# A pool of their own for the convolved rows, merge adds on VectorE, most weight roundings on ScalarE

## Chip, cores and metric

The kernel runs on one core of one Trainium2 chip. The metric is the device time of one execution in microseconds. The words used below: TensorE (PE in the rows, PEld its weight loads), VectorE (DVE), ScalarE (ACT), GpSimd (POOL) and SyncE's queue of transfers (SP).

## What is computed

One step of a trunk layer on 1088 frames (1024 of a prompt, 64 of a sample) of width 1024, in fp32. Four token mixers work side by side, their outputs are gated and added, and a gated feed-forward part with a causal convolution follows. The part that matters here:

```
p = x @ w_in + b_in                       # columns for the mixers A, B, C, D
mix = sum over m of sigmoid(x @ w_mg[m] + b_mg[m]) * (y_m @ w_br[m])
x1 = layer_norm(ALPHA * x + mix @ w_out)
gate = x1 @ w_ff_gate ; up = x1 @ w_ff_up          # 1024 -> 2048
ffn = (gelu(causal_dwconv3(gate)) * up) @ w_ff_down
x2 = layer_norm(ALPHA * x1 + ffn)
```

## The kernel before

**Weights.** Each fp32 product is made of three products of rounded parts: high by high, high by low, low by high (`mm3`, L293). The 184 weight tiles of 512 KB are listed in `plan` in the order of use, with a key each: `in` (48, the projection), `mg` (32, the gates of the merge), `br` (16, the branches), `out` (8), `fg` and `fu` (32, feed-forward gate and up) and `fd` (48, down). `wissue` (L246) loads a tile into `wr` (two buffers) on SyncE's queue, rounds it to `wh` (three buffers), and VectorE forms the remainder `wl` (L262). The rounding is on ScalarE for `fg` and `fu` (L259), on GpSimd for all others (L261).

**Merges.** The mixers run in the order D, C, B, A, each followed by its merge (`merge`, L672). Gates come out of TensorE as `psd` and ScalarE takes their tanh into `th` (L668). Then a tile `br` gives `psm` (two banks), and VectorE forms `(th + 1) * psm` in three pieces (L703). From the second merge on, the sum of the earlier mixers is loaded into `prev` and GpSimd adds it (L705), 24 times in all. After the last merge the sum is turned into the rounded parts `mixh` and `mixl` for the output projection (L1457, L1458).

**Feed-forward.** The columns are taken as 16 tiles `f` of 128. Tiles 0 and 1 are made plainly: gates (`ff_gate`), the convolution (`conv`, L1559 to L1567, into a tile `cv`), then the up products, which `put_up` multiplies into `cv` straight from the banks (L1547) and stores to `h_d`. For tiles 2 to 15, two at a time, `pair` (L341) replaces eight products of half matrices by seven. It needs sums of blocks of `x1` (`xsums`, L322: four sums `xs`, each as a rounded part on ScalarE at L338 and a remainder on VectorE at L339, per slice `k` of four) and sums of the weights (`wsums`, L269: `st`, `sh`, `sl`). The last 320 columns of each tile, `rest` (L357), and the first two products need no sums. All of it is on line L354 in the rows.

**What sets the order.** The program is written as generators that a tile scheduler orders; each engine then works through its list in order. Tiles come from pools; a tile waits until what used its memory before is done. `slot_pool` closes the pool of the slots and opens a new one in the same memory; here it opens the pools of the sums (`x`, `w`, `p`) beside seven slots, after the up tiles of `f` = 0 and 1.

Of the kernel before, what the change touches and what calls it, by code (L numbers as in the profile page):

```python
# [19 lines left out]
P = 128  # L20
# [48 lines left out]
def trunk_kernel(ctx: ExitStack, tc: tile.TileContext, I, O, dbg=None):  # L69
# [39 lines left out]
    def nm(s):  # L109
        uid[0] += 1  # L110
        return f"{s}_{uid[0]}"

    def slot(shape=(P, T), dt=F32, s="t"):
        return slots[1].tile(list(shape), dt, tag="T", name=nm(s))
# [4 lines left out]
    def bank(tag, n=512):  # L119
        return ps1.tile([P, n], F32, tag=tag, name=nm("ps" + tag))  # L120
# [125 lines left out]
    def wissue(upto, pin=False):  # L246
        while wptr[0] <= min(upto, len(plan) - 1):
            key, ap, a = plan[wptr[0]]
            pool = wide["f"] if key[0] == "fd" and key[1] > 2 and key[1] % 2 == 0 else wp
            raw = pool.tile([P, a, 1024 // a], F32, tag="wr", name=nm("wr"), bufs=2)  # L250
            pinned(SP.dma_start(raw, ap), pin)
            if key[0] == "out" and (key[1] == 1 or key[2] == 3):
                h = slot([P, a, 1024 // a], F32R, "woh")
                l = slot([P, a, 1024 // a], F32R, "wol")
            else:
                h = pool.tile([P, a, 1024 // a], F32R, tag="wh", name=nm("wh"), bufs=3)
                l = pool.tile([P, a, 1024 // a], F32R, tag="wl", name=nm("wl"), bufs=3)
            if key[0] in ("fg", "fu"):
                S.activation(h, raw, AF.Copy)  # L259
            else:  # L260
                G.tensor_scalar(h, raw, 1.0, 1.0, OP.mult, OP.mult)  # L261
            V.tensor_sub(l, raw, h.bitcast(F32))  # L262
            wtiles[key] = (h, l)
            wraw[key] = raw
            wptr[0] += 1
            if key in pairs:
                wsums(wraw.pop(pairs[key]), wraw.pop(key), key)
# [54 lines left out]
    def xsums():  # L322


        for j in (0, 1, 3):
            xs[j] = tuple(wide["x"].tile([P, 4, 384], F32R, tag=f"x{j}{i}", name=nm("xs"), bufs=1) for i in range(2))
        xs[2] = tuple(t[1][:, 0:4, :] for t in (xh, xl))

        for k in range(4):
            t, b12, b22, b21 = [wide["p"].tile([P, 384], F32, tag="xf", name=nm("xf"), bufs=5) for _ in range(4)]  # L330
            for v, c, kk in ((t, 0, k), (b12, 1, k), (b22, 1, k + 4), (b21, 0, k + 4)):
                V.tensor_tensor(v, xh[c][:, kk, :].bitcast(F32), xl[c][:, kk, :].bitcast(F32), OP.add)
            V.tensor_tensor(t, b12, t, OP.subtract)
            V.tensor_tensor(b12, b22, b12, OP.subtract)
            V.tensor_tensor(b22, b22, t, OP.subtract)
            V.tensor_tensor(b21, b21, b22, OP.subtract)
            for j, v in ((0, t), (1, b22), (3, b21), (2, b12)):
                S.activation(xs[j][0][:, k, :], v, AF.Copy)  # L338
                V.tensor_sub(xs[j][1][:, k, :], v, xs[j][0][:, k, :].bitcast(F32))  # L339

    def pair(ka, kb, add, put):  # L341

# [51 lines left out]
    def run(*gens):  # L394
        for g in gens:
            for _ in g:
                pass
# [274 lines left out]
    def merge(m, it):  # L672
# [19 lines left out]
        def br(e):  # L692
            wh, wl = wget(("br", m, e))
            for g in range(2):
                th = ths.pop((m, e + g))
                if it > 0:
                    prev = slot([P, T], F32, "prev")
                    SP.dma_start(prev, mx_d[it - 1][e + g])
                for c, (n0, n) in enumerate(CH):
                    ps = bank("m")  # L700
                    mm3(ps[:, :n], [(wh[:, k, g * P:(g + 1) * P], wl[:, k, g * P:(g + 1) * P],
                                     yh[k][:, n0:n0 + n], yl[k][:, n0:n0 + n]) for k in range(4)])
                    V.scalar_tensor_tensor(th[:, n0:n0 + n], th[:, n0:n0 + n], 1.0, ps[:, :n], OP.add, OP.mult)  # L703
                if it > 0:
                    G.tensor_tensor(th, th, prev, OP.add)  # L705
                if it < 3:
                    SP.dma_start(mx_d[it][e + g], th)
                else:
                    res.append(th)
# [785 lines left out]
    def x1done(tt, bb):  # L1495
        w = tw(tt)
        norm3(acc[tt], w, bb)
        SP.dma_start(x1_d[tt][0:w], acc[tt][0:w])

    seq = (0, 1, 2, 8, 3, 4, 5, 6, 7)  # L1500
    acc = [None] * NT
    l1g, l1b = None, None
# [51 lines left out]

    def conv(f):
        gp = gps.pop(f)
        cv = cvs[f] = slot(s="cv")
        for o, n, a in ((0, TP, 0), (TP, TS, TP + 2)):
            V.tensor_scalar(cv[:, o:o + n], gp[:, a:a + n], pk2[:, PK_FW + f:PK_FW + f + 1],  # L1559
                            pk2[:, PK_FB + f:PK_FB + f + 1], OP.mult, OP.add)  # L1560
# [36 lines left out]
    next(fg1)  # L1597
    xsplit(acc[7], 7)
    run(fg0, fg1)
    fu = []  # L1600
    for f in range(2):
        conv(f)
        fu.append(dense(("fu", f), lambda c, n0, n, ps, f=f: put_up(f, n0, n, ps), "m", (1, 0, 2), 2 - f))
        next(fu[f])
    run(*fu)
    slot_pool(7, "x", "w", "p")
    phase("G")
    xsums()
    for f in range(2, 16, 2):
        gate_pair(f)  # L1610
# [16 lines left out]
        return hi, lo  # L1627

    hcur = {(0, 0): h_tiles(0, 0)}
    pt = bank("m")  # L1630
    PE.transpose(pt[0:64, 0:P], stF.rearrange("p a b -> p (a b)"), ident)
    fo = small([64, P], "ffo", 1)
# [131 lines left out]
```

## Time and profile before

| | before |
|---|---|
| median of three runs | 2170.1 us (2170.0 to 2174.49) |
| profiled execution | 2169.9 us |
| its span | 2168.2 us |
| TensorE busy | 97% |
| VectorE busy | 54% |
| ScalarE busy | 29% |
| GpSimd busy | 19% |

The span is the time from the first to the last recorded instruction. A busy share is over the whole span. Waits are told by the instruction that waited and the one that released it. The granted clock is a share of full speed: 1.00 is 2.4 GHz, 0.50 is 1.2 GHz.

### The profile page before, as it was taken

The numbers are of one execution on the slowest core, as the hardware profiler recorded it, in microseconds if no ns is written. First come the engines' busy times: TensorE is split into PE (matmuls) and PEld (weight loads), VectorE is DVE, ScalarE is ACT, GpSimd is POOL, SyncE is SP. The second block draws the span as 40 slices with busy tenths as digits, with TensorE's granted clock in tenths as the row PEclk, the third lists the DMA queues.
The fourth block names the chain that finished last, engine by engine and source line by source line (L and its number), as shares of the span: only waits on it lengthen the run. The fifth ranks groups of instructions, "written<-read, shape, count | busy, mean of one in ns | idle before, by whom it ended". The sixth has DMA issues, their size and how long they took to land.

```text
span 2168.2 us, 31902 instructions
## 1 busy us (share of the span) xinstructions
PE 2105.0 (97%) x13035; PEld 1957.4 (90%) x13035; DVE 1170.2 (54%) x2174; ACT 633.8 (29%) x1173; POOL 410.6 (19%) x360
## 2 busy tenths in 40 slices
PE   8999999999999999999999999999996999999998
PEld 7999999888899888889999988997896999998886
DVE  5643346666433557545332245555556776667666
ACT  3753024545210244334201122311233333332110
POOL 1111001111123312210131102123210000003444
PEclk9999999999999999999999999999998999999999
DMA  5112221111143232132331212234211223237552
GB/s 152 51 60 91 95 71 39 45 44 44 45 152 122 79 100 75 56 90 60 124 133 58 70 38 67 74 124 159 78 68 37 80 70 91 61 97 284 202 211 102
DMA packets 193231, 200.31 MB, mean 92 GB/s; under 512 B 14588, under 2 KB 165448, under 8 KB 193084
## 3 DMA queue, kind: packets, MB, share of 16 engines
q1 hardware_dynamic: 193084, 198.26, 28.4%
q8 instruction: 103, 1.69, 0.3%
q14 instruction: 44, 0.36, 0.1%
HBM read 154.80 MB, written 43.43 MB: 91 GB/s over the span
## 4 chain that ended last, share of the span: by engine, by line
PE 81%; DVE 8%; issue 6%; POOL 2%; DMA 1%; ACT 1%; SPq 0%; DVEq 0%; POOLq 0%; ACTq 0%
PE psd L296 14%; PE psd L298 14%; PE psd L297 14%; PE pss L354 8%; PE pss L1674 3%; PE psm L296 3%; PE psm L297 3%; PE psm L298 3%; DVE wl L262 2%; PE psd L1674 1%; PE psm L1674 1%; PE psm L354 1%; PE pss L297 1%; PE pss L298 1%; PE pss L296 1%
## 5 line engine op out<-in xcount | busy, mean ns | idle before, releaser
L296 PE MATMUL psd<-xh,wh 128*128 128x384 f32 (+1 forms) x1920 | 642.2, 334 | 1.0 <-ACT xh L178 0.9
L298 PE MATMUL psd<-xh,wl 128*128 128x384 f32 (+1 forms) x1920 | 630.8, 329 | 0.0
L297 PE MATMUL psd<-xl,wh 128*128 128x384 f32 (+1 forms) x1920 | 629.4, 328 | 0.8 <-DVE xl L179 0.8
L262 DVE TENSOR_TENSOR wl<-wr,wh 128x1024 fp32r<-128x1024 f32 x179 | 263.0, 1475 | 333.8 <-POOL wh L261 272.1
L261 POOL TENSOR_SCALAR wh<-wr 128x1024 fp32r<-128x1024 f32 x147 | 170.8, 1164 | 1244.4 <-PE pss L354 364.3
L296 PEld LDWEIGHTS psd<-xh,wh 128*128 128x128 f32 x1920 | 362.4, 189 | 7.8 <-issue 3.0
L297 PEld LDWEIGHTS psd<-xl,wh 128*128 128x128 f32 x1920 | 361.1, 188 | 2.0 <-DVE xl L179 1.0
L298 PEld LDWEIGHTS psd<-xh,wl 128*128 128x128 f32 x1920 | 361.0, 188 | 0.5 <-DVE wl L262 0.3
L668 ACT ACTIVATE th<-psd,bhalf 128x384 f32<-128x384 f32 (+1 forms) x96 | 53.9, 562 | 343.3 <-PE psd L298 342.6
L296 PE MATMUL psm<-yh,wh 128*128 128x384 f32 (+1 forms) x384 | 126.5, 331 | 7.8 <-DVE th L703 7.8
L297 PE MATMUL psm<-yl,wh 128*128 128x384 f32 (+1 forms) x384 | 126.3, 329 | 0.3 <-DVE yl L688 0.3
L298 PE MATMUL psm<-yh,wl 128*128 128x384 f32 (+1 forms) x384 | 126.3, 329 | 0.0
L703 DVE SCALAR_TENSOR_TENSOR th<-th,psm 128x384 f32<-128x384 f32 (+1 forms) x96 | 50.4, 529 | 108.9 <-PE psm L298 107.7
L296 PE MATMUL psd<-x1h,wh 128*128 128x320 f32 (+1 forms) x272 | 85.2, 313 | 0.6 <-DVE x1l L189 0.6
L298 PE MATMUL psd<-x1h,wl 128*128 128x320 f32 (+1 forms) x272 | 84.9, 312 | 0.0
L297 PE MATMUL psd<-x1l,wh 128*128 128x320 f32 (+1 forms) x272 | 84.7, 312 | 0.0
L296 PEld LDWEIGHTS psm<-yh,wh 128*128 128x128 f32 x384 | 72.4, 189 | 10.4 <-DVE th L703 10.0
L1166 DVE CUSTOM_DVE_ANT_0 Pt<-pss,fcb 128x128 f32<-128x128 f32 (+7 forms) x64 | 48.1, 752 | 55.1 <-PE pss L1161 54.6
L259 ACT ACTIVATE wh<-wr 128x1024 fp32r<-128x1024 f32 x32 | 34.0, 1061 | 144.9 <-PE psd L297 46.9
L354 PE MATMUL pss<-xs,sh 128*128 128x384 f32 x224 | 59.1, 345 | 17.0 <-ACT sh L284 17.0
L297 PEld LDWEIGHTS psm<-yl,wh 128*128 128x128 f32 x384 | 72.6, 189 | 0.7 <-DVE yl L688 0.7
L298 PEld LDWEIGHTS psm<-yh,wl 128*128 128x128 f32 x384 | 72.6, 189 | 0.0
(535 smaller groups left out, 3901.8 us busy)
## 6 DMA issues: line engine op xcount, KB each, us to landing
wr<-in_w_in_dram SPq DMA_DIRECT2D x48, 512.0 KB
wr<-in_w_ff_down_dram SPq DMA_DIRECT2D x48, 512.0 KB
wr<-in_w_mg_dram SPq DMA_DIRECT2D x32, 512.0 KB
mx_d<-th SPq DMA_DIRECT2D x24, 544.0 KB
prev<-mx_d SPq DMA_DIRECT2D x24, 544.0 KB
wr<-in_w_br_dram SPq DMA_DIRECT2D x16, 512.0 KB
wr<-in_w_ff_gate_dram SPq DMA_DIRECT2D x16, 512.0 KB
wr<-in_w_ff_up_dram SPq DMA_DIRECT2D x16, 512.0 KB
```

The lines of the kernel that those rows point to most:

```text
L259: S.activation(h, raw, AF.Copy)
L261: G.tensor_scalar(h, raw, 1.0, 1.0, OP.mult, OP.mult)
L262: V.tensor_sub(l, raw, h.bitcast(F32))
L296: PE.matmul(ps, wh, mh, start=i == 0, stop=False)
L297: PE.matmul(ps, wh, ml, start=False, stop=False)
L298: PE.matmul(ps, wl, mh, start=False, stop=i == n - 1)
L354: PE.matmul(ps, w[:, k, :], x[:, k, :], start=start and k == 0 and i == 0, stop=k == 3 and i == 2, skip_group_check=not start)
L668: S.activation(th[:, n0:n0 + n], ps, AF.Tanh, bias=b, scale=0.5)
L703: V.scalar_tensor_tensor(th[:, n0:n0 + n], th[:, n0:n0 + n], 1.0, ps[:, :n], OP.add, OP.mult)
L1166: V.tensor_tensor_reduce(Pt[:, 0:L].rearrange("p (b n) -> p b n", b=nb), ps.rearrange("p (b n) -> p b n", b=2)[:, 0:nb, 0:n], cbs[hh][:, 0 ...
L1674: PE.matmul(ps[hf], a[:, f % 8, o:o + P], w[:, 0, sl], start=f == 0 and i == 0, stop=f == 15 and i == (2 if tt < 8 else 1))
```

## The change

It has four parts. The roundings of `mg`, `br`, `out` and `fd` (104 tiles) move from GpSimd to ScalarE; only `in` stays on GpSimd. The add of `th` and `prev` moves from GpSimd to VectorE. The `cv` tiles get a pool of their own with two buffers, opened ahead of the output projection; both plain convolutions come before the up tiles, and the pools of the sums open between the convolutions and the up tiles, beside four slots in place of seven. `xsums` makes the sums 0 and 1 for all four slices first and the sums 2 and 3 after them; one sum is rebuilt from its two parts, so that VectorE has 52 operations in place of 48.

```diff
@@ wissue
-            if key[0] in ("fg", "fu"):
+            if key[0] == "in":
+                G.tensor_scalar(h, raw, 1.0, 1.0, OP.mult, OP.mult)
+            else:
                 S.activation(h, raw, AF.Copy)
-            else:
-                G.tensor_scalar(h, raw, 1.0, 1.0, OP.mult, OP.mult)
             V.tensor_sub(l, raw, h.bitcast(F32))
@@ xsums
+        def temp(tag, c=None, k=None):
+            t = wide["p"].tile([P, 384], F32, tag=tag, name=nm(tag), bufs=4)
+            if c is not None:
+                V.tensor_tensor(t, xh[c][:, k, :].bitcast(F32), xl[c][:, k, :].bitcast(F32), OP.add)
+            return t
+
+        def parts(j, k, t):
+            S.activation(xs[j][0][:, k, :], t, AF.Copy)
+            V.tensor_sub(xs[j][1][:, k, :], t, xs[j][0][:, k, :].bitcast(F32))
+
+        t3 = []
         for k in range(4):
-            t, b12, b22, b21 = [wide["p"].tile([P, 384], F32, tag="xf", name=nm("xf"), bufs=5) for _ in range(4)]
-            for v, c, kk in ((t, 0, k), (b12, 1, k), (b22, 1, k + 4), (b21, 0, k + 4)):
-                V.tensor_tensor(v, xh[c][:, kk, :].bitcast(F32), xl[c][:, kk, :].bitcast(F32), OP.add)
-            V.tensor_tensor(t, b12, t, OP.subtract)
-            V.tensor_tensor(b12, b22, b12, OP.subtract)
-            V.tensor_tensor(b22, b22, t, OP.subtract)
-            V.tensor_tensor(b21, b21, b22, OP.subtract)
-            for j, v in ((0, t), (1, b22), (3, b21), (2, b12)):
-                S.activation(xs[j][0][:, k, :], v, AF.Copy)
-                V.tensor_sub(xs[j][1][:, k, :], v, xs[j][0][:, k, :].bitcast(F32))
+            b11, b12, b22 = temp("xf", 0, k), temp("xf", 1, k), temp("xf", 1, k + 4)
+            t3.append(temp("x3"))
+            V.tensor_tensor(b11, b12, b11, OP.subtract)
+            V.tensor_tensor(t3[k], b22, b12, OP.subtract)
+            V.tensor_tensor(b22, b22, b11, OP.subtract)
+            parts(0, k, b11)
+            parts(1, k, b22)
+        for k in range(4):
+            t2, b21 = temp("xf"), temp("xf", 0, k + 4)
+            V.tensor_tensor(t2, xs[1][0][:, k, :].bitcast(F32), xs[1][1][:, k, :].bitcast(F32), OP.add)
+            V.tensor_tensor(b21, b21, t2, OP.subtract)
+            parts(2, k, t3[k])
+            parts(3, k, b21)
@@ merge
-                    G.tensor_tensor(th, th, prev, OP.add)
+                    V.tensor_tensor(th, th, prev, OP.add)
@@ ahead of the output projection
+    wide["end"] = ExitStack()
+    wide["e"] = wide["end"].enter_context(tc.tile_pool(name="fe", bufs=2, side="right", reuse_waits="tile"))
@@ conv
-        cv = cvs[f] = slot(s="cv")
+        cv = cvs[f] = wide["e"].tile([P, T], F32, tag="cv", name=nm("cv"))
@@ feed-forward
     run(fg0, fg1)
+    conv(0)
+    conv(1)
+    slot_pool(4, "x", "w", "p")
+    phase("G")
     fu = []
     for f in range(2):
-        conv(f)
         fu.append(dense(("fu", f), lambda c, n0, n, ps, f=f: put_up(f, n0, n, ps), "m", (1, 0, 2), 2 - f))
         next(fu[f])
     run(*fu)
-    slot_pool(7, "x", "w", "p")
-    phase("G")
+    wissue(wpos["fg", 3])
     xsums()
@@ down projection
     hcur = {(0, 0): h_tiles(0, 0)}
+    wide["end"].close()
```

In the changed kernel the lines of `merge` are 14 higher (L703 is L717, L705 is L719) and those of the feed-forward functions 16 higher (L1547 is L1563); ScalarE's rounding is L261 there. The sums are L332 to L351, with L337 the remainder of `xs` or, for the sum 2, of `x1l`, whose memory it takes.

VectorE, at the end of the plain up tiles, before: `cv` with `psm` is an up eviction, `xf` and `xs` are the sums. The numbers behind a name tell one buffer from another.

```order
L262 TENSOR_TENSOR wl_15271<-wr_15268,wh_15270 128x1024
L1547 TENSOR_TENSOR cv_15014<-cv_15014,psm_15105 128x384
L1547 TENSOR_TENSOR cv_15014<-cv_15014,psm_15132 128x320
L332 TENSOR_TENSOR xf_15182<-x1h_14009,x1l_14010 128x384
L332 TENSOR_TENSOR xf_15183<-x1h_14011,x1l_14012 128x384
L332 TENSOR_TENSOR xf_15184<-x1h_14011,x1l_14012 128x384
L332 TENSOR_TENSOR xf_15185<-x1h_14009,x1l_14010 128x384
L333 TENSOR_TENSOR xf_15182<-xf_15183,xf_15182 128x384
```

The same engine after, from a piece among the up evictions to the sums behind the last one:

```order
L332 TENSOR_TENSOR xf_15220<-x1h_14009,x1l_14010 128x384
L332 TENSOR_TENSOR xf_15222<-x1h_14011,x1l_14012 128x384
L1563 TENSOR_TENSOR cv_14984<-cv_14984,psm_15125 128x384
L332 TENSOR_TENSOR xf_15224<-x1h_14011,x1l_14012 128x384
L343 TENSOR_TENSOR xf_15220<-xf_15222,xf_15220 128x384
L344 TENSOR_TENSOR x_2363_15226<-xf_15224,xf_15222 128x384
L332 TENSOR_TENSOR xf_15234<-x1h_14009,x1l_14010 128x384
L345 TENSOR_TENSOR xf_15224<-xf_15224,xf_15220 128x384
L337 TENSOR_TENSOR xs_15201<-xf_15220,xs_15200 128x384
L1563 TENSOR_TENSOR cv_14984<-cv_14984,psm_15152 128x320
L332 TENSOR_TENSOR xf_15236<-x1h_14011,x1l_14012 128x384
L332 TENSOR_TENSOR xf_15238<-x1h_14011,x1l_14012 128x384
```

Before, the first row of the sums stands behind the last eviction, and `st` and `sl` behind all of them. After, the evictions stand among the sums of the first slices (the last one here is the row with `psm_15152`), 18 rows ahead of the remainder of the second sum's last slice, and the first gate pair's `st` and `sl` have gone ahead of these rows.

VectorE in the second merge, around the remainder `wl_5844` of the next `br` weight, before:

```order
L703 SCALAR_TENSOR_TENSOR th_5065<-th_5065,psm_5797 128x384
L703 SCALAR_TENSOR_TENSOR th_5065<-th_5065,psm_5811 128x384
L703 SCALAR_TENSOR_TENSOR th_5065<-th_5065,psm_5825 128x320
L262 TENSOR_TENSOR wl_5844<-wr_5841,wh_5843 128x1024
L703 SCALAR_TENSOR_TENSOR th_5174<-th_5174,psm_5849 128x384
L703 SCALAR_TENSOR_TENSOR th_5174<-th_5174,psm_5863 128x384
```

GpSimd around the same add (`th_5065` with `prev_5795`) and the rounding ahead of that `wl` (`wh_5843`), before:

```order
L705 TENSOR_TENSOR th_4926<-th_4926,prev_5749 128x1088
L261 TENSOR_SCALAR wh_5843<-wr_5841 128x1024
L705 TENSOR_TENSOR th_5065<-th_5065,prev_5795 128x1088
L705 TENSOR_TENSOR th_5174<-th_5174,prev_5847 128x1088
L261 TENSOR_SCALAR wh_5942<-wr_5940 128x1024
```

VectorE at the same place after:

```order
L717 SCALAR_TENSOR_TENSOR th_4926<-th_4926,psm_5779 128x320
L719 TENSOR_TENSOR th_4926<-th_4926,prev_5749 128x1088
L717 SCALAR_TENSOR_TENSOR th_5065<-th_5065,psm_5797 128x384
L717 SCALAR_TENSOR_TENSOR th_5065<-th_5065,psm_5811 128x384
L717 SCALAR_TENSOR_TENSOR th_5065<-th_5065,psm_5825 128x320
L719 TENSOR_TENSOR th_5065<-th_5065,prev_5795 128x1088
L262 TENSOR_TENSOR wl_5844<-wr_5841,wh_5843 128x1024
L717 SCALAR_TENSOR_TENSOR th_5174<-th_5174,psm_5849 128x384
L717 SCALAR_TENSOR_TENSOR th_5174<-th_5174,psm_5863 128x384
```

The add stands on VectorE now, between the last piece of a `th` tile and the next `wl`; GpSimd has neither the add nor the rounding, which stands on ScalarE (L261).

## Rows read from the trace of the kernel before

**Rows 1.** The page, busy time: engine, us, share of the span, instructions.

```profile
PE 2105.0 (97%) x13035; PEld 1957.4 (90%) x13035; DVE 1170.2 (54%) x2174; ACT 633.8 (29%) x1173; POOL 410.6 (19%) x360
```

**Rows 2.** TensorE's waits: who waited for whom, us in all, times, longest.

```profile
PE pss L354 <- ACT sh L284: 17.0, 1, 17.0
PE psm L296 <- DVE th L703: 7.8, 7, 2.1
...
PE pss L297 <- DVE wl L262: 1.3, 1, 1.3
...
PE pss L354 <- ACT wh L259: 0.3, 1, 0.3
```

**Rows 3.** Windows around the longest wait: busy us by engine, granted clock, DMA.

```profile
core 0: us, PE busy (x) PEld busy (x) DVE busy (x) ACT busy (x) POOL busy (x), PEclk, DMA share, GB/s
...
1645.00:1650.00 5.00, 5.00 (x36) 5.00 (x35) 2.94 (x7) 1.18 (x4) 0.00 (x0) 1.00 0.00 0
...
1665.00:1670.00 5.00, 1.55 (x4) 1.04 (x5) 4.74 (x13) 1.06 (x1) 0.00 (x0) 0.50 0.00 0
1670.00:1675.00 5.00, 5.00 (x20) 5.00 (x18) 2.65 (x4) 1.23 (x2) 0.00 (x0) 0.59 0.63 169
```

**Rows 4.** VectorE's timeline, up tiles and sums: start, us, instruction, idle before.

```profile
1626.38 0.56 DVE L1547 TENSOR_TENSOR cv<-cv,psm 128x384 f32<-128x384 f32 x1 [1.18 <-ACT cv L1567]
...
1640.01 0.49 DVE L1547 TENSOR_TENSOR cv<-cv,psm 128x320 f32<-128x320 f32 x1 [2.96 <-PE psm L298]
1640.41 1.96 DVE L332 TENSOR_TENSOR xf<-x1h,x1l 128x384 f32<-128x384 f32 x4
...
1664.84 0.55 DVE L339 TENSOR_TENSOR xs<-xf,xs 128x384 fp32r<-128x384 f32 x1
1665.31 0.68 DVE L278 TENSOR_TENSOR st<-wr 128x512 f32<-128x512 f32 x1
...
1668.18 1.23 DVE L285 TENSOR_TENSOR sl<-st,sh 128x1024 fp32r<-128x1024 f32 x1 [0.23 <-ACT sh L284]
```

**Rows 5.** GpSimd's timeline in the second merge: one add.

```profile
628.93 2.53 POOL L705 TENSOR_TENSOR th<-th,prev 128x1088 f32<-128x1088 f32 x1
```

**Rows 6.** VectorE's timeline in the first merge (one row) and the second.

```profile
267.60 1.23 DVE L262 TENSOR_TENSOR wl<-wr,wh 128x1024 fp32r<-128x1024 f32 x1 [0.43 <-POOL wh L261]
...
627.94 0.49 DVE L703 SCALAR_TENSOR_TENSOR th<-th,psm 128x320 f32<-128x320 f32 x1 [1.21 <-PE psm L298]
629.00 3.54 DVE L262 TENSOR_TENSOR wl<-wr,wh 128x1024 fp32r<-128x1024 f32 x1 [0.56 <-POOL wh L261]
632.46 1.01 DVE L703 SCALAR_TENSOR_TENSOR th<-th,psm 128x384 f32<-128x384 f32 x2
```

**Rows 7.** TensorE's timeline: after three waits in merges, and before the sums.

```profile
633.06 0.41 PE L296 MATMUL psm<-yh,wh 128*128 128x320 f32 x1 [0.95 <-DVE th L703]
...
1482.64 0.41 PE L296 MATMUL psm<-yh,wh 128*128 128x320 f32 x1 [2.12 <-DVE th L703]
...
1490.52 0.50 PE L297 MATMUL pss<-wl,mixh 128*128 128x512 f32 x1 [1.34 <-DVE wl L262]
...
1641.92 0.33 PE L354 MATMUL psm<-x1h,wh 128*128 128x384 f32 x1
...
1644.00 0.31 PE L296 MATMUL psd<-x1h,wh 128*128 128x320 f32 x1
...
1647.51 0.31 PE L296 MATMUL psd<-x1h,wh 128*128 128x320 f32 x1
```

**Rows 8.** What GpSimd's 24 adds with `prev` waited for: us, times.

```profile
  DVE th L703: 54.1, 10
  PE psm L298: 4.3, 1
```

**Rows 9.** Windows at the end of the last merge, columns as in rows 3.

```profile
1480.00:1485.00 5.00, 2.88 (x13) 2.56 (x13) 4.46 (x7) 1.39 (x4) 1.04 (x1) 0.80 0.35 99
1485.00:1490.00 5.00, 4.17 (x17) 3.25 (x16) 3.58 (x2) 0.59 (x3) 4.16 (x3) 0.86 0.03 9
```

**Rows 10.** Roundings by line: count, busy us, mean ns, idle before.

```profile
L261 POOL TENSOR_SCALAR wh<-wr 128x1024 fp32r<-128x1024 f32 x147 | 170.8, 1164 | 1244.4 <-PE pss L354 364.3 <-issue 292.3 <-PE psd L297 266.1
...
L259 ACT ACTIVATE wh<-wr 128x1024 fp32r<-128x1024 f32 x32 | 34.0, 1061 | 144.9 <-PE psd L297 46.9 <-PE pss L298 40.8 <-DMA wr<-in_w_ff_up_dram 30.0
```

## The prediction

> **What bounds the kernel now.** TensorE is busy 2105.0 us, 97% of the 2168.2 us span [rows 1]; the profiled execution took 2169.9 us, 0.2 below the median of 2170.1. So nothing off TensorE matters unless TensorE waits for it, and I read the table of its waits first [rows 2]. One wait stands out: 17.0 us, once, for the weight sums `sh` in the feed-forward stage. Next come 7.8 us in seven waits for the merge's `th` on VectorE, and 1.3 us for a weight remainder `wl`. A change elsewhere moves little.
>
> The windows around the long wait show its second price [rows 3]: TensorE's granted clock is 1.00 (2.4 GHz) before, and 0.50 (1.2 GHz) and 0.59 in the two windows in which the work is taken up. From 1668.2 to 1670 half of 1.8 us is lost, and 0.41 x 5 in the next window: 0.9 + 2.05 = 2.95 us. The stall costs 17.0 + 2.95 = 20.0 us.
>
> Why it waits is in VectorE's own timeline [rows 4]. The 48 operations of `xsums` start at 1640.41, right behind the last eviction of the plain up tiles at 1640.01, because they stand behind it in program order. They run to 1665.3, 0.47 us apart; only then come the weight sums `st` (1665.31) and the remainder `sl` (1668.18).
>
> The waits in the merges: on GpSimd the add of `th` and `prev` starts at 628.93 and takes 2.53 us [rows 5]; VectorE's `wl`, begun at 629.00, takes 3.54 us. In the first merge, which has no such add, a `wl` takes 1.23 us [rows 6]. The next `th` of VectorE then starts at 632.46, and TensorE, with both banks full, resumes 0.95 us late [rows 7]. The longest of the seven waits is the 2.12 us at 1482.64; the six others are of the size shown, 7.8 - 2.1 = 5.7 us in all.
>
> **The sums move forward.** The new order puts the evictions of the six up chunks among the sums, so that VectorE fills what was idle (1.18 us before the row at 1626.38, 2.96 before the one at 1640.01, and so on) [rows 4]. I walked TensorE's and VectorE's new rows side by side with durations of the trace. A product matmul of TensorE follows the next after 0.173 us (12 from 1641.92 to 1644.00), a dense one of 320 columns after 0.146 (24 to 1647.51) [rows 7]. TensorE now does four product matmuls between the up chunks, so the up tiles end 0.7 later than before, at 1640.5; the other 20 products (3.5) and a dense block of 24 (3.5) follow, to 1647.5. Then it needs the second pair of sums, slice by slice, and the remainder of the last slice after 10 products and 4 dense matmuls (2.3), at 1649.8. VectorE has 18 rows from the last eviction (done 1641.2) to that slice: 18 x 0.47 = 8.5, so 1649.7. The last slice of the third sum is needed after 14 products, 20 dense matmuls and 12 products more (7.4), at 1657.2, and VectorE has it 16 rows later: 7.5, so also 1657.2. A `wl` behind it is 0.5 to 0.7 late. Thus two needs are met with nearly no slack and one is missed by a little; I put 1.5 us of new waiting, in pieces under a microsecond, and no fall of the clock: the shortest wait of these rows behind which it fell is the one of 2.12 us [rows 7, 9]. Bounds: 0; and 8, if TensorE could only go on after all 52 sums: 52 x 0.47 = 24.4 us and 9.6 of other work (five `st` at 0.68, two `sl` and a `wl` at 1.23, five evictions at 0.5) from 1625.2 end at 1659.2, 8 behind the 1651.2 (1668.2 - 17.0) at which work without sums ran out. Gain: 20.0 - 1.5 = 18.5.
>
> The price of the four added operations (52 for 48) is inside this walk. The `cv` tiles now have two buffers and a convolution waits for the stores of the tile two before; the only new waiter is VectorE, which has idle stretches there; I cost it at nothing.
>
> **The add on VectorE.** It has no row there. Its bounds are a two-input operation of 128x1024 alone, 1.23 [rows 6], and GpSimd's own 2.53 [rows 5]; the first is the same engine and kind, so 1.23 x 1088/1024 = 1.3. The step at 628: the last `th` piece of a tile ends at 628.4 (627.94 + 0.49), the add at 629.7, `wl` at 630.9 instead of 632.5. That is 1.5 us earlier where 0.95 was missing, so all six waits go: 5.7 us. At 2.53 `wl` would end at 632.2, and only 0.3 of each 0.95 would be won, 1.8 us. The add now makes VectorE wait for the load of `prev`, with the next tile's `th` queued behind it and TensorE's banks behind that; but in the trace the adds waited only for `th` and a bank, not for this load [rows 8], so I cost it at nothing.
>
> At the end of the last merge the chain is the same with the projection's weights: 2.12 us of wait, 1.34 for `wl` [rows 7], and a half-clock spell, (0.20 + 0.14) x 5 = 1.7 us [rows 9]. Together 5.2. With the 3.55 of `wl` back at 1.23 most goes, but each add now stands ahead of the conversions for the projection on VectorE, so I take 4 (2 to 5.2).
>
> First the rows: the add kept its 2.53 us and `wl` took its own 1.2 on top, which is one operation after the other, not two slowed ones. The Trainium skill (SBUF — State Buffer, Who interferes with whom) says so too, an exclusive lock; but the Trainium skill (Perfetto Trace Analysis, Optimizing Scalar/DVE Operations) warns that moving operations between GpSimd and VectorE, which share a read port, might not help. By that warning the merges keep their 5.7 and 5.2 us; by the rows VectorE's time per step falls from 3.54 to 2.5. The warning is rival 2.
>
> **The roundings on ScalarE.** 104 of GpSimd's roundings (1164 ns) become ScalarE's (1061 ns for the same tile) [rows 10]. ScalarE is busy 29% of the span [rows 1] and did 32 such roundings already; TensorE waited for them 0.3 us in all [rows 2]. Behind a rounding on ScalarE stand the tanh evictions of the gates; the cover is the dense work that TensorE still has open banks for. I cost it at nothing, bounds 0 to 0.5 us each of the 56 that fall outside the down projection, which is rival 4.
>
> **The sum.** 18.5 + 5.7 + 4 = 28.2 off 2169.9: 2141.7; from the median 2142. All ends favourable (20.0 + 5.7 + 5.2) give 2139; all unfavourable but with no rival (12 + 1.8 + 2) give 2154.
>
> **The rivals.** (1) VectorE's backlog becomes the new bound of the feed-forward stage: two needs meet with no slack, and a wait there also delays the loads' buffers. Against it: the idle stretches among the up tiles [rows 4]. Eight us of new wait instead of 1.5: 2148. (2) The add helps nothing, VectorE being held as long as before: only 18.5 remain, 2151. Against it: the `wl` of 1.23 in the merge without an add [rows 6]. (3) The change does not do what it says, the sums still ending last because some buffer is freed by the up tiles; only the merges gain: 2169.9 - 9.7 = 2160. Against it: the order itself. (4) Slower: a rounding waits on ScalarE for its load or for TensorE to leave the buffer, and holds tanh evictions until TensorE's banks are full. For it: ScalarE sat idle 144.9 us before the 32 roundings of now, 46.9 of it for TensorE [rows 10]. It decides from 28.2/56 = 0.5 us each; at 0.7 the time is 2169.9 - 28.2 + 39 = 2181.
>
> **How the numbers follow.** Forecast (2139 to 2146): 0.63. Rival 1: 0.12. Rival 2: 0.07. Rival 3: 0.05. Rival 4: 0.04. Better than 2139, because GpSimd's roundings were also holding up VectorE in places that I did not price: 0.06. Several of the new waits together, with nothing left of the gain: 0.03. A range of 2137 to 2153 takes in the forecast, rivals 1 and 2 and a part of the better case, 0.84. Faster by over 0.2% (4.3 us, about what a measurement of this kernel can tell from no change) are all but the last case and rival 4: 0.93; within, 0.03; slower, 0.04.
>
> **What would show it.** Right: no wait of TensorE for `sh` over 2 us and a granted clock of 1.00 throughout the feed-forward stage; the sums' first operations between up evictions; the add at about 1.3 us on VectorE, every `wl` in the merges at 1.23; TensorE's waits for `th` gone. Wrong: a wait for `xs`, `x1l` or `wl` of several us at the first gate pair (rival 1), `th` still waited for (rival 2), or TensorE waiting for tanh on ScalarE in the gates (rival 4). The number falls if the walk's zero slack turns into a second idle stretch long enough for the clock.

## The result and the profile after

The changed kernel takes 2141.8 us (median of four runs, 2141.2 to 2144.8) against 2171.8 us for the kernel before (four runs beside it): a ratio of 0.9864, interval 0.9847 to 0.9881, so 30.0 us less. The two profiled executions, 2141.45 and 2169.9 us, differ by 28.45; the sum of the prediction was 28.2. Its time, 2142, and its range, 2137 to 2153, held.

The page's busy times after, to be read against [rows 1]:

```profile
span 2139.7 us, 31840 instructions
...
PE 2101.1 (98%) x13035; PEld 1955.5 (91%) x13035; DVE 1151.5 (54%) x2202; ACT 737.1 (34%) x1277; POOL 223.7 (10%) x232
```

TensorE does the same 13035 matmuls. VectorE has 28 operations more (24 adds, four in the sums) and yet 18.7 us less busy time, because operations that stood beside GpSimd's are shorter. The groups of the remainders and the add (count, busy us, mean ns, then the idle time ahead of them) show it. The first line is of before: the mean of `wl` was 1475 ns there and is 1248 ns now, near the 1.23 us of the undisturbed one in [rows 6], and the add has 1332 ns.

```profile
L262 DVE TENSOR_TENSOR wl<-wr,wh 128x1024 fp32r<-128x1024 f32 x179 | 263.0, 1475 | 333.8 <-POOL wh L261 272.1 <-ACT wh L259 47.6 <-PE psm L1075 10.6
...
L262 DVE TENSOR_TENSOR wl<-wr,wh 128x1024 fp32r<-128x1024 f32 x179 | 222.7, 1248 | 327.6 <-ACT wh L261 202.5 <-POOL wh L259 106.1 <-PE psm L1089 10.6
...
L719 DVE TENSOR_TENSOR th<-th,prev 128x1088 f32<-128x1088 f32 x24 | 32.0, 1332 | 0.8
```

TensorE's waits after, as in [rows 2] (us in all, times, longest). The 17.0 for `sh` and the 7.8 for `th` are gone. What leads now, 8.3 for `vt`, lies in the mixer's transposes, which the change did not aim at.

```profile
PE psm L957 <- DVE vt L961: 8.3, 4, 3.3
...
PE psm L297 <- DVE yl L702: 1.4, 2, 0.7
```

The windows of the feed-forward stage and, in the last two rows, of the end of the last merge, columns as in [rows 3]. Where [rows 3] had TensorE busy 1.55 of 5 us at a granted clock of 0.50, and [rows 9] 2.88 at 0.80, TensorE is busy 5 of 5 at 1.00 (2.4 GHz); 4.93 is the worst window.

```profile
1640.00:1645.00 5.00, 5.00 (x31) 4.80 (x30) 5.00 (x12) 2.76 (x7) 0.00 (x0) 1.00 0.00 0
...
1650.00:1655.00 5.00, 4.93 (x30) 4.60 (x29) 5.00 (x11) 1.69 (x5) 0.00 (x0) 1.00 0.02 5
1480.00:1485.00 5.00, 5.00 (x23) 3.93 (x22) 4.75 (x7) 2.52 (x6) 0.00 (x0) 1.00 0.28 98
1485.00:1490.00 5.00, 5.00 (x24) 4.06 (x23) 2.61 (x3) 1.06 (x1) 0.00 (x0) 1.00 1.01 340
```

VectorE's timeline at the same place as [rows 4], a few rows of the walk. The sums and the weight sums `st` stand among the up evictions from 1617 on; the last eviction starts at 1633.02, and the remainder on which the second product waits longest ends at 1641.9, 8.4 us behind the eviction's end.

```profile
1617.52 0.69 DVE L278 TENSOR_TENSOR st<-wr 128x512 f32<-128x512 f32 x1
...
1633.02 0.49 DVE L1563 TENSOR_TENSOR cv<-cv,psm 128x320 f32<-128x320 f32 x1
...
1641.38 0.57 DVE L337 TENSOR_TENSOR xs<-xf,xs 128x384 fp32r<-128x384 f32 x1
...
1649.97 1.25 DVE L262 TENSOR_TENSOR wl<-wr,wh 128x1024 fp32r<-128x1024 f32 x1
```

TensorE in these microseconds. Before the last slice's remainder is there it goes on with other work (the dense `psd` rows at 1641.62), and at 1642.20 takes the slice up with no wait in its row.

```profile
1641.62 0.31 PE L296 MATMUL psd<-x1h,wh 128*128 128x320 f32 x1
...
1642.20 0.34 PE L368 MATMUL pss<-xs,sh 128*128 128x384 f32 x1
```

VectorE in the second merge, the place of [rows 6]: eviction, add, remainder, one behind the other, without the 3.54.

```profile
631.82 0.49 DVE L717 SCALAR_TENSOR_TENSOR th<-th,psm 128x320 f32<-128x320 f32 x1 [1.21 <-PE psm L298]
632.34 1.29 DVE L719 TENSOR_TENSOR th<-th,prev 128x1088 f32<-128x1088 f32 x1
633.55 1.22 DVE L262 TENSOR_TENSOR wl<-wr,wh 128x1024 fp32r<-128x1024 f32 x1
```

**Where the time went, by stretch.** I cut each profiled execution at four of TensorE's rows that every kernel has: the end of its work ahead of the first wait for `vt`, ahead of the wait for `fko`, ahead of the third wait for `mn`, and ahead of the first gate matmul of the feed-forward stage. The distances in us:

| kernel | start to first `vt` | to `fko` | to third `mn` | merges, to feed-forward | feed-forward to end |
|---|---|---|---|---|---|
| before | 347.3 | 360.0 | 199.9 | 681.6 | 579.4 |
| after | 350.1 | 358.6 | 199.8 | 672.2 | 559.0 |
| after once more | 350.9 | 361.1 | 199.8 | 671.9 | 558.8 |
| E1, add alone | 348.8 | 360.8 | 199.7 | 672.2 | 579.4 |
| E2, roundings alone | 350.7 | 365.6 | 199.9 | 677.9 | 579.0 |
| E3, feed-forward part alone | 348.8 | 360.0 | 199.9 | 679.4 | 560.3 |

The change gains 20.4 us in the feed-forward stretch, 9.4 in the merges and 1.4 ahead of `fko`, and gives back 2.8 at the start. Of these, 1.8 lie where the input is loaded (TensorE's wait for `xl` begins at 21.4 in place of 19.6). The change touches nothing there, and in the other runs, none of which touches it either, this point lies between 19.9 and 22.5: it is the load that varies. The other 1.0 is in part a wait of 0.71 for `yl` at 195, at the start of the first merge. Two executions of the changed kernel differ by 2.5 us ahead of `fko`; the last section comes to that.

The theory that went into the experiments: the feed-forward gain is the stall of [rows 2] and the clock behind it, removed because the sums run among the up tiles; the merge gain is the add, off GpSimd, no longer doubling VectorE's `wl`; the roundings are neutral. The rivals: the roundings carry part of the merge gain, since GpSimd is freed by them too; the new order inside `xsums` carries the feed-forward gain, not the pool; and the zero slack of the walk is real, or was never there.

### The profile page after: what moved, and what is told of

It is laid out like the page before. It is cut to its first block, busy times and chain, and to the rows that moved or that the text cites. A ratio compares the mean times of both kernels' runs of the same rounds, so it can differ in the third digit from the quotient of the medians.

```text
span 2139.7 us, 31840 instructions
## 1 busy us (share of the span) xinstructions
PE 2101.1 (98%) x13035; PEld 1955.5 (91%) x13035; DVE 1151.5 (54%) x2202; ACT 737.1 (34%) x1277; POOL 223.7 (10%) x232
## 4 chain that ended last, share of the span: by engine, by line
PE 51%; DVE 2%; DMA 1%; ACT 0%; issue 0%; POOL 0%; SPq 0%; DVEq 0%; ACTq 0%
PE pss L368 8%; PE psd L296 7%; PE psd L298 7%; PE psd L297 7%; PE pss L1693 5%; PE psd L1693 2%; PE psm L1693 2%; PE psm L297 2%; PE psm L296 2%; PE psm L298 2%; PE pss L296 1%; PE pss L297 1%; PE pss L298 1%; PE psm L368 1%; PE psm L1330 1%; PE psm L1117 0%
## 5 line engine op out<-in xcount | busy, mean ns | idle before, releaser
L262 DVE TENSOR_TENSOR wl<-wr,wh 128x1024 fp32r<-128x1024 f32 x179 | 222.7, 1248 | 327.6 <-ACT wh L261 202.5
L261 ACT ACTIVATE wh<-wr 128x1024 fp32r<-128x1024 f32 x131 | 139.0, 1061 | 376.6 <-PE psd L297 127.5
L259 POOL TENSOR_SCALAR wh<-wr 128x1024 fp32r<-128x1024 f32 x48 | 52.7, 1098 | 669.7 <-PE psd L297 266.5
L717 DVE SCALAR_TENSOR_TENSOR th<-th,psm 128x384 f32<-128x384 f32 (+1 forms) x96 | 50.9, 531 | 104.5 <-PE psm L298 103.2
L1496 POOL TENSOR_TENSOR lrs<-lrs,mhalf 128x1 f32<-128x1 f32 (+1 forms) x16 | 9.8, 614 | 665.9 <-ACT hh L1640 423.9
```

## The experiments

**E1: the add alone on VectorE.** The kernel before, with

```diff
-                    G.tensor_tensor(th, th, prev, OP.add)
+                    V.tensor_tensor(th, th, prev, OP.add)
```

> The kernel before with one edit: the 24 adds of th and prev go from GpSimd to VectorE; roundings stay on GpSimd. My theory: the merge gain hangs on the add alone, because GpSimd's 2.53 us add held the remainder wl at 3.54 us. So wl takes 1.23 us in the merges, the add about 1.29, TensorE's wait for th falls from 7.8 us to under 1, the half-clock spell at the end of the last merge goes, and the time is about 10 us below the kernel before (2160 to 2163). The rival, that the roundings on GpSimd were what slowed VectorE, expects no more than 2 us of gain and wl still long. The 17 us wait for sh stays in both.

Measured: 2162.7 us (2160.2 to 2164.1), ratio 0.9961 [0.9949, 0.9974]. The merge stretch has all of the 9.4 us (table above), and the wait for `th` is down from 7.8 to one of 0.3. From the second wait for `vt` to the one for `fko` it takes 292.4 us against 295.0 of before, so the two merge steps there are won as well; that the table shows 360.8 for the whole stretch is due to the longer first wait for `vt` (3.4 here), to which the last section comes.

```profile
PE pss L354 <- ACT sh L284: 17.0, 1, 17.0
PE psm L943 <- DVE vt L947: 8.4, 4, 3.4
...
PE pss L297 <- DVE wl L262: 1.0, 1, 1.0
```

The long wait for `sh` is untouched, to the tenth. The add is worth 2.6 + 9.4 = 12 us in the merges, and needs no other part for that; the median moved by 8.0, and the profile by 7.3, the rest being eaten by the start (1.5) and the first wait for `vt` (3.4).

**E2: the roundings alone on ScalarE.** The kernel before, with

```diff
-            if key[0] in ("fg", "fu"):
+            if key[0] == "in":
+                G.tensor_scalar(h, raw, 1.0, 1.0, OP.mult, OP.mult)
+            else:
                 S.activation(h, raw, AF.Copy)
-            else:
-                G.tensor_scalar(h, raw, 1.0, 1.0, OP.mult, OP.mult)
```

> The kernel before with one edit: the 104 roundings of mg, br, out and fd go from GpSimd to ScalarE; the add stays on GpSimd. My theory: no gain by itself; the seven waits for th stay (5 to 8 us), wl stays at 3.5 us in the merges, and what is new is a loss of 1 to 3 us at the merges' starts and ahead of the second merge: time 2171 to 2175, within 0.2% of the kernel before. The rival, that the roundings are a part of the merges' gain, expects 3 us or more below the kernel before.

Measured: 2170.5 us (2168.6 to 2176.5, 11 runs), ratio 1.000 [0.999, 1.001]: nothing, as a sum. But not nothing place by place. The waits for `th` were to stay at 5 to 8 us and fell to 4.6, and two other waits grew:

```profile
PE psm L943 <- DVE vt L947: 10.1, 4, 3.4
PE psm L296 <- DVE th L703: 4.6, 7, 1.0
...
PE psm L297 <- DVE yl L688: 1.0, 2, 0.7
```

The longest `th` wait, 2.12 in [rows 7], is 0.50 here, and the merge stretch is 3.7 us shorter. What is won there is lost in this profile at `vt` (10.1 against 6.8 before: 3.37 at 350.7, of which more at the end, and 3.31 at 549.8, against 1.54 and 1.78) and at the start of the merges. In the whole change the add alone would take nearly all the `th` waits, so that this gain is there once, not twice; the losses at 549.8 (546 in after) and at the merge starts stay (E8).

**E3: the feed-forward part alone** (the pool for `cv`, the earlier pools of the sums, the new `xsums`). The kernel after, with the add on GpSimd and the roundings as before.

> The kernel before with the feed-forward part of the change alone (the pool for cv, the pools of the sums opened with the up tiles, the new order of the sums). Theory: the 17 us wait for sh is gone with its half-clock spell, new waits there are under 1 us, TensorE's 7.8 us for th stay: 20 us below the kernel before, 2151 to 2153. If the parts of the change need each other, the gain is clearly smaller than 20 us, or larger.

Measured: 2152.5 us (2150.0 to 2154.9), ratio 0.9916 [0.9902, 0.9929]. The feed-forward stretch is 19.1 us shorter, the waits for `th` stay at 7.7. The 1.3 us by which its feed-forward stretch stays behind that of the whole change are two waits of TensorE for VectorE: 0.65 us at 1945 for `pp`, in the last pair of tiles, and 0.71 at 2034 for a `wl`, in the down projection. After has one of 0.2 in their place, before one of 0.6:

```profile
PE psd L1693 <- DVE wl L262: 0.7, 1, 0.7
PE pss L368 <- DVE pp L1599: 0.6, 1, 0.6
```

In the whole change they are gone or nearly so. For the `wl` the roundings do it: E1 keeps that wait at 0.6, E2 has 0.2. Which of their properties does it is not shown.

**E5: the new order of the sums alone.** The kernel before with the new `xsums`, the `cv` tiles in slots and the pools of the sums opened where they were, beside six slots in place of seven (the new sums need more memory).

```diff
-    slot_pool(7, "x", "w", "p")
+    slot_pool(6, "x", "w", "p")
     phase("G")
     xsums()
```

> The kernel before with the new order of the sums alone; cv stays in the slots, of which there are six in place of seven, since the longer-lived x3 tiles need the room. Theory: what held the sums back is the memory that the up tiles still use, so the first sum still starts behind the last up eviction, the weight sums still come behind all 52 operations, and the wait for sh stays at 15 to 20 us: the time is within 3 us of the kernel before. The rival, that making the sums 0 and 1 first is what pays, expects TensorE to go on 16 operations earlier, a wait of about 9 us and a gain of 7 or more.

Measured: 2174.1 us (2170.9 to 2177.0, ten runs), ratio 1.0015 [1.0006, 1.0024]: a little slower, with the wait as it was. What the order costs and what the slot less costs is not told apart here.

```profile
PE pss L368 <- ACT sh L284: 17.4, 1, 17.4
```

**E4: the whole change with the old order of the sums**, the counterpart: `xsums` as before, all else as after.

> The changed kernel with the old order of the sums (all four sums of a slice together, 48 operations). Theory: the pool does the work; the scheduler puts the second dense block ahead of the sums' products, so TensorE still finds work while VectorE is 15 us behind the last up eviction, and the time is within 2 us of the changed kernel. The rival, that the new order of the sums is needed, expects a wait of about 5 us for xs at the first gate pair and 5 us or more above the changed kernel.

Measured: 2143.5 us (2142.9 to 2145.9), ratio 0.9860 [0.9844, 0.9877]. Its feed-forward stretch is 560.0 us against 559.0 of after; no wait for a sum is left in its table. E5 and E4 together: the new pools do the work, and the new order of the sums inside is worth about 1 us of the stretch with them (the medians of E4 and of after on the same chip are only 0.1 apart) and nothing without. The new pools are here one bundle: the pool for `cv`, both convolutions first, the pools of the sums opened ahead of the up tiles, four slots and the one weight tile issued early. No run takes it apart.

**After once more**, on the chip of E4 and E6.

> The changed kernel once more, as the yardstick of the three that follow. 2141 to 2143 us.

Measured: 2143.4 us (2139.7 to 2144.3), ratio 0.9858 [0.9843, 0.9872], its stretches for the merges and the feed-forward stage 671.9 and 558.8.

**E6: VectorE's step in the merge made longer.** The kernel after, with one operation more behind each add (its result isn't used):

```diff
                     V.tensor_tensor(th, th, prev, OP.add)
+                    V.tensor_tensor(prev, prev, prev, OP.add)
```

> The changed kernel with a second operation of the same size on VectorE behind each of the 24 adds (prev plus prev, into prev, whose result nothing uses). Theory: in the steps with a wl VectorE has 0.6 to 0.8 us of slack, so 1.29 us more brings back 0.4 to 0.7 us of TensorE's wait for th in each of the six or seven steps: 3 to 5 us above the changed kernel, waits for th of 2.5 to 5 us in all. If VectorE has plenty of slack in the merges, nothing changes; if the add is on TensorE's path everywhere, 24 x 1.29 = 31 us come back.

Measured: 2145.1 us (2142.3 to 2148.9), ratio 0.9870 [0.9855, 0.9884]. The 3 to 5 us are not there: the median is 1.7 above that of after on the same chip, with intervals that overlap, the merge stretch of its profile is 671.4 us, as in after, and no wait for `th` is in its table. VectorE's step is longer by 1.2 us (the row at 635.87):

```profile
633.52 1.29 DVE L719 TENSOR_TENSOR th<-th,prev 128x1088 f32<-128x1088 f32 x1
...
635.87 1.28 DVE L720 TENSOR_TENSOR prev<-prev 128x1088 f32<-128x1088 f32 x1
637.07 1.01 DVE L717 SCALAR_TENSOR_TENSOR th<-th,psm 128x384 f32<-128x384 f32 x2
```

TensorE, at the place where it would have waited for the bank, does four dense matmuls (`psd`) first, 0.70 us of work:

```profile
636.84 0.34 PE L298 MATMUL psm<-yh,wl 128*128 128x384 f32 x1
637.01 0.34 PE L296 MATMUL psd<-xh,wh 128*128 128x384 f32 x1
...
637.54 0.34 PE L296 MATMUL psd<-xh,wh 128*128 128x384 f32 x1
637.71 0.38 PE L296 MATMUL psm<-yh,wh 128*128 128x320 f32 x1
```

The order of the program is recorded anew for each kernel, and the scheduler put independent work there. So a price worked out on the old order of TensorE's rows can be an upper end only. E4 shows the same: its sums are made in the old order, but 24 dense matmuls stand among its first products of the sums, where after has 4.

**E7: less slack in the sums.** The kernel after, with the third sum's subtraction done three times for each slice, 8 operations of 0.47 us more, 3.8 us:

```diff
             V.tensor_tensor(t3[k], b22, b12, OP.subtract)
+            V.tensor_tensor(t3[k], b22, b12, OP.subtract)
+            V.tensor_tensor(t3[k], b22, b12, OP.subtract)
```

> The changed kernel with each of the four x3 subtractions done three times over (the same result), 8 operations of 0.47 us more in the sums. Theory: VectorE has next to no slack between the plain up tiles and the first gate pair, so 8 x 0.47 = 3.8 us come out as 3 to 4 us of new waiting of TensorE there, and 3 to 4 us of time. If the stage has slack (TensorE's dense blocks can be put ahead of more), the time moves by less than 1 us.

Measured: 2147.4 us (2144.2 to 2151.7), ratio 0.9880 [0.9865, 0.9895]; the feed-forward stretch is 562.7 us against 558.8 and 559.0, 3.8 more: all of the added work. TensorE waits in four pieces, 3.1 us together. The first two are for the second pair of sums, where the walk of the prediction had put a need without slack; the other two are for ScalarE's evictions of banks behind them:

```profile
1647.64 0.45 PE L370 MATMUL pss<-xs,sh 128*128 128x384 f32 x1 [0.75 <-ACT xs L336]
...
1648.49 0.44 PE L370 MATMUL pss<-xs,sh 128*128 128x384 f32 x1 [0.41 <-DVE xs L337]
...
1651.79 0.45 PE L370 MATMUL pss<-x1h,sh 128*128 128x384 f32 x1 [0.58 <-ACT pp L380]
...
1655.65 0.42 PE L296 MATMUL psd<-x1h,wh 128*128 128x320 f32 x1 [1.38 <-ACT gp L1561]
```

The granted clock stays at 1.00 in the three windows from 1645 to 1660, with TensorE busy 3.7 to 4.4 of each 5 us. The order was recorded anew here too, with 24 dense matmuls among the first products as in E4, and it did not hide the added work. So zero slack is real: the changed kernel takes its sums just in time.

**E8: the roundings of the merges back on GpSimd.** The kernel after, with

```diff
-            if key[0] == "in":
+            if key[0] in ("in", "mg", "br"):
```

> The changed kernel with the roundings of mg and br back on GpSimd; those of out and fd stay on ScalarE. Theory: with the add off GpSimd its roundings cost the merges nothing, and the two small losses that came with ScalarE's roundings go: the waits for yl and yh at two merges' starts (2 us) and the 1.5 us ahead of the second merge (3.3 back to 1.8). So 1 to 3.5 us below the changed kernel in the stretch up to the feed-forward stage, and no wait for th. The rival, that GpSimd's later start of these roundings makes wl late again, expects waits for th of 1 us or more in all.

Measured: 2139.2 us (2137.1 to 2140.6), ratio 0.9857 [0.9843, 0.9870]. The wait at 546 us is back from 3.32 to 1.78, and one of the two waits for `yl` is gone:

```profile
PE psm L957 <- DVE vt L961: 6.7, 4, 1.8
...
PE psm L297 <- DVE yl L702: 0.7, 1, 0.7
```

From the second wait for `vt` to that for `fko` it takes 292.5 us against 293.6 in after: 1.1 won of the 1.5. The span of its profile is 0.8 us shorter, and the median 2.6 below that of after. But the kernels before beside them differ by as much (2170.2 here, 2171.8 and 2173.1 beside the two runs of after), and the ratio of 0.9857 lies within the intervals of after's 0.9864 and 0.9858. So a gain of the whole is not shown; the rows alone agree with its sign.

**E9: the products of the mixer on VectorE.** What leads the waits after is `vt`, and beside it stand GpSimd's two products `qR` and `kU` (L947 and L949 in its lines, 2.3 and 2.2 us each on average), four times. The kernel after, with both on VectorE behind the copies of `vt`:

```diff
-        G.tensor_tensor(blk(qR), blk(qc), eR[:, 0:34].unsqueeze(2).to_broadcast([P, 34, 32]), OP.mult)
...
-        G.tensor_tensor(blk(kU), blk(kc), eU[:, 0:34].unsqueeze(2).to_broadcast([P, 34, 32]), OP.mult)
         vt, kt = slot([P, 9, P], s="vt"), slot([P, 9, P], s="kt")
         for src, dst, eng in ((vT, vt, 0), (kU, kt, 1)):
+            if eng:
+                V.tensor_tensor(blk(kU), blk(kc), eU[:, 0:34].unsqueeze(2).to_broadcast([P, 34, 32]), OP.mult)
+                V.tensor_tensor(blk(qR), blk(qc), eR[:, 0:34].unsqueeze(2).to_broadcast([P, 34, 32]), OP.mult)
```

> The changed kernel with the two scalings qR and kU of the third mixer (8 operations of 128x1088 on GpSimd, 2 us each alone) on VectorE, behind the copies of vt. What it asks: whether the 8.3 us for vt, and the step of about 3.4 us by which profiles of one kernel differ near 350 us, come from GpSimd's operation and VectorE's wl or KX starting within 0.1 us of each other. If so, the waits for vt fall below 4 us, no wait of 3.4 us near 350 is seen, and the time is 4 to 9 us below the changed kernel. If VectorE becomes the bound there, TensorE waits for kU or qR instead and the time does not move.

Measured: 2131.7 us (2130.6 to 2132.1), ratio 0.9822 [0.9809, 0.9835], 10 us below after. By the ratios, each to the kernel before on its own chip, it is 8 to 9 us, the upper end of what was expected. Its profile is 9.7 us shorter than that of after, and 9.5 of them are won ahead of `fko`. All four waits for `vt` are gone, and VectorE does at the fourth place in 1.3 us each what took 2.0 us each on GpSimd:

```profile
541.26 1.27 DVE L950 TENSOR_TENSOR kU<-z,eU 128x1088 f32<-128x1088 f32 x1
542.46 1.28 DVE L951 TENSOR_TENSOR qR<-qc,eR 128x1088 f32<-128x1088 f32 x1
```

**E10: E8 and E9 together.**

> Both edits together, the roundings of mg and br on GpSimd and the two scalings on VectorE. If they are independent, the sum of their gains: 5 to 12 us below the changed kernel, 2130 to 2137. If they are not, as much as the better of the two.

Measured: 2131.4 us (2131.0 to 2131.5), ratio 0.9821 [0.9808, 0.9835]: the same as E9, though the waits for `yl` have left its table. E9 and E10 beat both kernels of this case.

## Why the prediction was right, step by step

- **The stall and its clock, 20.0.** Right: the feed-forward stretch is 20.4 us shorter. The accounts close to about half a microsecond: 20.0, less 0.1 of new waiting, and 0.5 more from the down projection, where the wait for `wl` is 0.17 in place of 0.63. For E3 they close too: 20.0 - 0.1, less the 0.65 and the 0.1 by which its two waits there are longer, is 19.15 against 19.1. (A wait of 0.3 for `wh` [rows 2] and one of 0.25 for `sl` behind the stall went too; they had no term.) One reading of the prediction was incomplete: the 48 sums before are not all 0.47 us apart, one waits 2.06 us for a rounding on ScalarE, at 1648.65. Nothing in the sum hangs on it.
- **New waiting, 1.5.** Mis-sized, 0.07 measured (one gap, at 1651.2, ahead of the product that needs the `wl` of 1649.97). The walk itself was right on both engines: from 1639.71 TensorE does 10 products, 4 dense matmuls, 14 products, 20 dense and the next products of the sums, as counted, and VectorE's remainder ends 8.4 us behind the eviction where 8.5 was worked out. What was too big is the size put on top of it. The walk had found one miss, of 0.5 to 0.7 us for that `wl`, and 1.5 was taken; the third sum's last slice was there about 0.3 us ahead of its product (1649.34 against 1649.69), and most of the miss went with that. Rival 1, eight us of backlog, did not come; E7 shows how near it lies, since every added microsecond came back.
- **What moved the sums.** The prediction told it as one step, the sums going forward. E5 and E4 split it: the cause lies in the new pools, the order inside `xsums` is only 1 us of it. In the program's text `xsums()` stands behind the up tiles in both kernels; what came earlier is the memory for the sums. So the mechanism of rival 3, sums held back by memory of the up tiles, was that of the kernel before, and the change removed it. TensorE's wait was for `sh` alone; no run moved the weight sums without the other sums, so how much of the 20 us that would have brought is open.
- **The add, 5.7 in six merge steps.** The mechanism was right: 1.29 us where 1.3 was worked out, `wl` at 1.22, no wait for `th` left, and E1 alone does it. The size was too small. Two steps lie ahead of `fko` and gave 2.6 us in E1, 1.3 each in place of 0.95. The wait in the table is not the whole price of a step, and TensorE's rows before, on both sides of the one at 633.06 [rows 7], show most of the rest:

```profile
631.78 0.33 PE L298 MATMUL psm<-yh,wl 128*128 128x384 f32 x1
...
633.31 0.31 PE L297 MATMUL psm<-yl,wh 128*128 128x320 f32 x1
```

  A row is 0.33 us long, but the next one of its kind starts 0.17 behind it, and the table counts from a row's end. The row at 633.06 should have started at 631.95, and the one behind it came 0.25 later in place of 0.146: 1.11 + 0.10 = 1.2 us. Rival 2 fell with the same rows. The Trainium skill (Perfetto Trace Analysis, Optimizing Scalar/DVE Operations) warns that such a move might not help. Here it did, for this operation and in this direction, with 3.54 us becoming 1.22.
- **The end of the last merge, 4 of 5.2.** Mis-sized: all 5.2 are won. In E1 the `th` wait there is 0.3 and the clock full, but 1.0 us of waiting for `wl` is left; in after both waits are gone. That is not the roundings' doing for sure: E3, with add and roundings as before, has 0.28 for that `wl` where before had 1.34. The adds that I feared ahead of the conversions hold up no one: TensorE is busy 5.00 of 5 in both windows.
- **The sum.** Its closeness owes something to luck: the feed-forward stretch and the merges brought 20.4 + 9.4 + 2.5 = 32.3 where 28.2 were worked out, and costs that had no term took back 1.1 at 546 and 2.8 at the start, most of that from the load of the input. It also owes something to the execution that was profiled: the other one of the changed kernel has a span of 2142.5, 25.7 us below before.
- **The roundings at nothing.** Right in the sum (E2: 1.000), wrong as a description. They shorten the `th` waits by 3.2 us where the add is still on GpSimd (E2), they remove about half a microsecond in the down projection (E1, E2), and they cost 1.1 us at 546 and some tenths at the start of the first merge (0.71 for `yl` at 195, gone in E8). The 0.70 for `yl` at 1054, where before had 0.35, stays in E8, so it isn't theirs. The reason at 546 shows in the rows of VectorE and GpSimd in after:

```profile
545.91 2.08 POOL L949 TENSOR_TENSOR kU<-z,eU 128x1088 f32<-128x1088 f32 x1
...
546.51 2.03 DVE L984 TENSOR_TENSOR KX<-z,EX 128x512 f32<-128x512 f32 x1 [0.39 <-ACT EX L935]
548.47 0.68 DVE L961 COPY vt<-psm 128x512 f32<-128x512 f32 x1
549.07 0.67 DVE L984 TENSOR_TENSOR KX<-z,EX 128x512 f32<-128x512 f32 x1
```

  `KX` takes 2.03 us beside GpSimd's `kU` and 0.67 alone, and in the new order one of them stands ahead of the first copy of `vt`, for which TensorE waits 3.32. In E8 the copy comes ahead of both, as in before, and TensorE waits 1.78. Here TensorE didn't wait for tanh on ScalarE, so rival 4 was the wrong mechanism for a cost that did exist.
- **Better than 2139 because GpSimd's roundings held up VectorE elsewhere (0.06).** It did not come. What holds up VectorE elsewhere are GpSimd's products, which stayed where they were; E9 shows that these places are worth 8 to 10 us.

## What to carry to other kernels

When work that depends on nothing late still runs late, look at which pool's memory it waits for before looking at its order: here the new pools were worth the stall, the order 1 us. In this kernel a two-input fp32 operation on GpSimd was paid twice, by its own length (2.53 us for the add, 1.29 on VectorE) and by what VectorE lost beside it (`wl` at 3.54 in place of 1.23). It was cheaper on VectorE, which had room, in both places where it was moved (E1, E9). A price worked out on the old order can be an upper end if a scheduler writes a new one; but slack worked out to be zero is worth a run that adds work, since nothing in the profile shows how near the next stall is.

## What the runs showed of the hardware

**Two starts 0.05 us apart, and a step of 3.4 us.** At the first `vt` wait GpSimd's `qR` and VectorE's `wl` start almost together, 0.05 us apart, in before and in E1 alike. In before GpSimd's operation is the long one and TensorE waits 1.54:

```profile
346.83 3.15 POOL L933 TENSOR_TENSOR qR<-qc,eR 128x1088 f32<-128x1088 f32 x1 [3.07 <-DVE qc L901]
...
346.88 1.22 DVE L262 TENSOR_TENSOR wl<-wr,wh 128x1024 fp32r<-128x1024 f32 x1
...
348.85 0.27 PE L943 MATMUL psm<-ident,vT 128*64 128x128 f32 x1 [1.54 <-DVE vt L947]
```

In E1 VectorE's is, with the same starts, and TensorE waits 3.37:

```profile
348.35 2.02 POOL L933 TENSOR_TENSOR qR<-qc,eR 128x1088 f32<-128x1088 f32 x1 [3.07 <-DVE qc L901]
...
348.40 3.05 DVE L262 TENSOR_TENSOR wl<-wr,wh 128x1024 fp32r<-128x1024 f32 x1
...
352.20 0.40 PE L943 MATMUL psm<-ident,vT 128*64 128x128 f32 x1 [3.37 <-DVE vt L947]
...
351.00:356.00 5.00, 3.80 (x14) 3.83 (x15) 3.95 (x7) 0.00 (x0) 2.33 (x1) 0.66 0.38 105
```

The last line is the window behind it: the granted clock is 0.66, between the two levels of 1.2 and 2.4 GHz. From this wait to the next one it is 68.4 us in place of 65.0. E2, E4 and E5 show the 3.37 too, before, after, after again, E3, E6, E7 and E8 the 1.54. The Trainium skill (SBUF — State Buffer, Who interferes with whom) has VectorE and GpSimd share an exclusive lock for which the order of issue decides who blocks. The rows agree with the lock: one operation keeps its own length and the other takes nearly both (3.15 and 3.05 where 2.02 + 1.22 is 3.24). They don't show what decides, since by the profile GpSimd's operation starts 0.05 us ahead in both. That this is also why runs of one kernel spread over 3 us or so is likely, not shown: E9, which has no such pair, spreads over 1.5 us.

**The same wait dropped the clock in one execution and not in another.** In after, TensorE waits 3.32 us for `vt`, until 549.20, and the granted clock stays at 1.00 (2.4 GHz). After once more is the same program: its rows keep a distance of 0.8 us to those of after from 352 on, it waits the same 3.32 us, until 549.95, and the window behind it has 0.50 (1.2 GHz). The first line is of after, the second of after once more:

```profile
549.00:554.00 5.00, 4.80 (x30) 4.77 (x31) 1.53 (x4) 0.29 (x1) 0.00 (x0) 1.00 0.00 0
...
549.00:554.00 5.00, 4.05 (x13) 4.05 (x14) 2.29 (x5) 0.00 (x0) 0.00 (x0) 0.50 0.00 0
```

From there on its rows are 2.4 us further behind. E6 and E7 wait 3.32 at this place too and have 0.66 in the same window. In before, 2.12 us at the end of the last merge were enough for 0.80 [rows 9]. So neither the length of the wait nor the work ahead of it tells, in these runs, whether the clock falls; what does is not shown. It also means that the wait that E8 shortens costs 1.1 us against one profile of the changed kernel and 3.5 against the other (292.5 us from the second `vt` to `fko`, against 293.6 and 296.0).
